# The output projection and the routing in a written order, and the first expert's weights behind the lists

## The chip, the cores and the metric

The kernel runs on one core of a Trainium2 chip. The metric is the device time of one execution in microseconds; a version is timed in several runs and their median is used. One further execution was recorded by the hardware profiler, and all rows here come from it.

## The reference

One transformer block over 1024 tokens of width 1024, in float32. The part that matters here is its end:

```python
x = x + merged @ w_out                                   # output projection
t = rms_norm(x, norm_ffn)                                # 1024 tokens
group_logits = t @ w_rg + b_rg                           # 4 groups
...                                                      # best group, softmax over its 8 experts, top 2
out = 0
for e in range(32):
    hidden = silu(t @ w_gate[e]) * (t @ w_up[e])         # width 256
    out = out + combine[:, e:e + 1] * (hidden @ w_down[e])
x = x + out
```

Each token goes to two of the 32 experts, so only these rows of `combine` are not zero.

## The kernel before

Products are made in three passes of a split float32: an operand is split into a high part (a ScalarE copy, L81) and a low part (a VectorE subtraction, L82), and `mm3` (L85 to L87) multiplies high by high, high by low and low by high.

The attention stages end with the merged branches, split, in `mT` (four pairs of buffers of the `ring`). Then the stage of this change follows, in eight token tiles `t` of 128 rows. `out_mm` projects a tile: two column halves `c`, eight steps `k` each, so 48 matmuls in all, then `x` is added (L884) and the sum `x2` stored to `out`. `w_out` comes in eight slabs `wo[k]`; the last four are loaded and split by `load_wo` shortly before. `route` squares and sums `x2` on ScalarE, takes the power -1/2 on GpSimd (L108), writes the normed rows `h2` to memory (L896, L897), transposes `x2` (L902), multiplies by the router's weights (L909), and then finds the group and the two experts in some 25 small VectorE steps and two exponentials on ScalarE. `place` counts with two small matmuls how many earlier tokens chose each expert (L959, L960) and adds the tile's entries into the slot table `psL` by two matmuls with a selection matrix `sl` (L965 to L969). After the last tile `slot_lists` makes from `psL` the lists: `ids`, the token numbers in each expert's 112 slots, and the weights `wsl`.

The experts then run one after the other. `gather` fetches an expert's rows of `h2` by an indirect DMA on GpSimd's queue into a buffer `gbuf`; four such buffers are filled with zeros first, by ScalarE (L1013). `tokens` transposes and splits the rows, `gate_up`, `hidden_t` and `down` compute, and `down` ends with an indirect DMA that adds into `out`. An expert's weights are six slabs of 512 KB, split by `weights`. They are loaded ahead: five slabs in buffers `er`, then pairs in the eight `ring` buffers as `mT` comes free after each second tile. A slab's buffer is loaded again when its low part has been made. After expert 2 a block of small VectorE steps (`ext`, `cum`, L1128 to L1141) prepares a loop over overfull experts at the end.

The order on each engine is made by the framework's scheduler from dependencies and the place in the source; engines take their queues in order, and the loads are all issued by SyncE's queue.

Of the kernel before, what the change touches and what calls it, by code (L numbers as in the profile page):

```python
# [10 lines left out]
F32 = mybir.dt.float32  # L11
# [12 lines left out]
NT = 8  # L24
# [23 lines left out]
def kernel(ctx: ExitStack, tc: tile.TileContext, a, out):  # L48
# [19 lines left out]
    def bank2():  # L68
        return psA.tile([P, 1024], F32, name="pA", tag="pA")
# [10 lines left out]
    def split(hi, lo, src, eng=None):  # L80
        nc.scalar.activation(hi, src, AF.Copy)  # L81
        (eng or nc.vector).tensor_tensor(lo, src, hi, op=ALU.subtract)  # L82
# [787 lines left out]
    X2 = {}  # L870

    def out_mm(t, k0, k1):
        if k0 == 0:
            xr = rt("xr", [P, D])
            nc.sync.dma_start(xr, a["x"][t * P:(t + 1) * P, :])
            X2[t] = (xr, bank2())
        xr, ps = X2[t]
        for c in range(2):
            o = slice(c * 512, (c + 1) * 512)
            for k in range(k0, k1):  # L880
                c_ = slice(k * P, (k + 1) * P)
                mm3(ps[:, o], mT[t // 2][0][:, t % 2, c_], mT[t // 2][1][:, t % 2, c_], wo[k][0][:, o], wo[k][1][:, o], k == 0, k == KD - 1)
            if k1 == KD:
                nc.vector.tensor_tensor(xr[:, o], ps[:, o], xr[:, o], op=ALU.add)  # L884
        if k1 == KD:
            nc.sync.dma_start(out[t * P:(t + 1) * P, :], xr)
            X2[t] = xr

    def route(t):
        x2 = X2.pop(t)  # L890
        h2 = rt("h2", [P, D])
        ss = rt("ss2", [P, 1])
        nc.scalar.activation(h2, x2, AF.Square, accum_out=ss)
        r = rt("r2", [P, 1])
        rstd(r, ss, D)
        nc.vector.scalar_tensor_tensor(h2, x2, r, gffn, op0=ALU.mult, op1=ALU.mult)  # L896
        nc.sync.dma_start(h2_d[t * P:(t + 1) * P, :], h2)  # L897
        xt = rt("xt", [P, D])
        for g in range(2):
            pt = bank()  # L900
            for k in range(4):
                nc.tensor.transpose(pt[:, k * P:(k + 1) * P], x2[:, (4 * g + k) * P:(4 * g + k + 1) * P], ident)  # L902
            if g:
                nc.vector.tensor_copy(xt[:, 512:], pt)
            else:
                nc.scalar.activation(xt[:, :512], pt, AF.Copy)
        pl = bank("g")
        for k in range(KD):
            nc.tensor.matmul(pl[:, :40], xt[:, k * P:(k + 1) * P], wrr[:, k, :], start=k == 0, stop=k == KD - 1)  # L909
# [10 lines left out]
        nc.vector.tensor_scalar(gb, gm[:, 0:1], -1.0, None, op0=ALU.mult)  # L920
        ge = rt("ge", [P, NG])
        gs = rt("gs", [P, 1])
        nc.scalar.activation(ge, lg[:, :NG], AF.Exp, bias=gb, accum_out=gs)
        sel = rt("sel", [P, NE])
        nc.vector.tensor_scalar(sel, iog, gif, NEG, op0=ALU.not_equal, op1=ALU.mult)
# [9 lines left out]
        nc.scalar.activation(ex, dl, AF.Exp)  # L935
# [5 lines left out]
        E = rt("E", [P, 2, NE])  # L941
        nc.vector.tensor_tensor(E, slots[:, None, :NE].to_broadcast([P, 2, NE]),
                                eid[:, t, :, None].to_broadcast([P, 2, NE]), op=ALU.is_equal)
# [5 lines left out]
        RT[t] = (E, L)  # L949

    RT = {}

    def place(t):

        E, L = RT.pop(t)
        M = rt("M", [P, NE], BF16)
        nc.vector.tensor_tensor(M, E[:, 0, :], E[:, 1, :], op=ALU.add)
# [3 lines left out]
        nc.vector.tensor_tensor(mcum, mcum, M, op=ALU.add)  # L961
# [10 lines left out]
    for t in range(2):  # L972
        out_mm(t, 0, 4)
    for i in range(N_RAW):
        load([er(i)])
    for t in range(2):
        out_mm(t, 4, KD)
    load_pairs(2)
    for t in range(NT):
        if 1 < t + 1 < NT:  # L980
            out_mm(t + 1, 0, KD)
            if t % 2 == 0:
                load_pairs(2)
        route(t)
        if t:
            place(t - 1)
    place(NT - 1)

    def slot_lists(ps, n, nm):


        idf = cst.tile([P, n], F32, name=f"idf{nm}")
        nc.vector.tensor_scalar(idf, ps[:, 3 * n:4 * n], ndump, dump, op0=ALU.mult, op1=ALU.add)
        ids = cst.tile([P, n], I32, name=f"ids{nm}")
        nc.vector.tensor_tensor(ids, ps[:, :n], idf, op=ALU.add)
# [5 lines left out]
    ids, wsl = slot_lists(psL, NE, "")  # L1001
    pn = bank()
# [41 lines left out]
    def tokens(e):  # L1044
# [6 lines left out]
        split(xh, xl, pt.rearrange("p (k n) -> p k n", n=P)[:, :, :BT])  # L1051
        XT[e] = (xh, xl)

# [55 lines left out]
    weights(0, 0, 6)  # L1109
    tokens(0)  # L1110
    for e in range(NE + 1):
# [7 lines left out]
        if e + 1 < NE:  # L1119
            weights(e + 1, 4, 6)  # L1120
            tokens(e + 1)
        if e:
            down(e - 1, col(ids, e - 1), col(wsl, e - 1))
        if e == 2:

            NB = 2 * S // BT + 1
            ext = pe.tile([P, NE], F32, name="ext")
            nc.vector.tensor_scalar(ext, cnt, float(BT), None, op0=ALU.is_gt)  # L1128
            for b in range(2, -(-S // BT)):
                nc.vector.scalar_tensor_tensor(ext, cnt, float(b * BT), ext, op0=ALU.is_gt, op1=ALU.add)  # L1130
            cum = [pe.tile([P, NE], F32, name=f"cum{i}") for i in range(2)]
            nc.vector.tensor_copy(cum[0], ext)
            for i, w_ in enumerate((1, 2, 4, 8, 16)):
                src, dst = cum[i % 2], cum[(i + 1) % 2]
                nc.vector.tensor_copy(dst[:, :w_], src[:, :w_])
                nc.vector.tensor_tensor(dst[:, w_:], src[:, w_:], src[:, :NE - w_], op=ALU.add)
            cm_ = cum[1]
            nbi = pe.tile([P, 1], I32, name="nbi")
            nc.vector.tensor_copy(nbi, cm_[:, NE - 1:NE])
            jc = pe.tile([P, 1], F32, name="jc")  # L1140
            nc.vector.memset(jc, 0.0)  # L1141
# [115 lines left out]
```

## Time and profile before

| | us |
|---|---|
| median of 3 runs | 1284.02 (1281.01 to 1285.81) |
| the profiled execution, its time | 1276.85 |
| its span, first to last instruction | 1275.1 |
| output projection and routing, TensorE full | 779 to 888 |
| end of the routing, lists, first gather | 888 to 911 |
| experts | 911 to 1275 |

Times in the rows are microseconds from the span's start. PE is TensorE, PEld its weight load, DVE VectorE, ACT ScalarE, POOL GpSimd, SPq SyncE's queue. A line L82 is line 82 of the kernel; helpers such as the split are used from many places, and the names of the tiles tell them apart.

### The profile page before, as it was taken

The numbers are of one execution on the slowest core, as the hardware profiler recorded it, in microseconds if no ns is written. First come the engines' busy times: TensorE is split into PE (matmuls) and PEld (weight loads), VectorE is DVE, ScalarE is ACT, GpSimd is POOL, SyncE is SP. The second block draws the span as 40 slices with busy tenths as digits, with TensorE's granted clock in tenths as the row PEclk, the third lists the DMA queues.
The fourth block names the chain that finished last, engine by engine and source line by source line (L and its number), as shares of the span: only waits on it lengthen the run. The fifth ranks groups of instructions, "written<-read, shape, count | busy, mean of one in ns | idle before, by whom it ended". The sixth has DMA issues, their size and how long they took to land.

```text
span 1275.1 us, 18222 instructions
## 1 busy us (share of the span) xinstructions
PE 1166.7 (92%) x6105; PEld 941.1 (74%) x6105; DVE 937.7 (74%) x2083; ACT 735.6 (58%) x1376; POOL 168.5 (13%) x147
## 2 busy tenths in 40 slices
PE   7789999989999999999998999999499898989994
PEld 6678888868888886777776878887377665657763
DVE  4587694368888788888764775545699788879982
ACT  6344463257667666776663443212488677668882
POOL 1000000010000001110100000000252443332112
PEclk9889999999999999999999999999599899999997
DMA  8853375383332333441215444555689999999983
GB/s 278 182 182 116 108 198 162 112 181 86 89 92 75 92 94 97 116 118 40 67 58 198 134 147 171 188 194 181 209 265 327 311 306 312 317 313 350 344 308 52
DMA packets 107615, 228.62 MB, mean 179 GB/s; under 512 B 13984, under 2 KB 47392, under 8 KB 107520
## 3 DMA queue, kind: packets, MB, share of 16 engines
q1 hardware_dynamic: 86272, 201.98, 47.7%
q0 software_dynamic: 21248, 25.46, 9.6%
q8 instruction: 49, 0.80, 0.3%
q14 instruction: 46, 0.38, 0.1%
HBM read 187.53 MB, written 52.43 MB: 188 GB/s over the span
## 4 chain that ended last, share of the span: by engine, by line
PE 49%; DMA 29%; DVE 12%; ACT 5%; issue 3%; SPq 1%; POOL 0%; POOLq 0%; ACTq 0%; DVEq 0%
DMA ring<-in_w_exp 12%; DMA er<-in_w_exp 7%; PE pG L85 6%; PE pG L86 5%; PE pG L87 5%; PE pA L85 3%; PE pB L528 3%; PE pA L86 3%; PE pA L87 3%; DMA sgl<-g_d 2%; PE pO L87 2%; PE pO L85 2%; PE pO L86 2%; DVE nbd L516 2%; PE pA L664 1%
## 5 line engine op out<-in xcount | busy, mean ns | idle before, releaser
L82 DVE TENSOR_TENSOR elo<-ring,ehi 128x1024 fp32r<-128x1024 f32 x120 | 142.4, 1220 | 16.2 <-ACT ehi L81 15.3
L81 ACT ACTIVATE ehi<-ring 128x1024 fp32r<-128x1024 f32 x120 | 124.8, 1058 | 34.7 <-DMA ring<-in_w_exp 18.3
L519 ACT ACTIVATE pd<-pA,nbd 128x512 f32<-128x512 f32 (+7 forms) x128 | 94.6, 740 | 37.8 <-DVE nbd L516 34.6
L85 PE MATMUL pG<-ring,whi 128*128 128x512 f32 x240 | 99.9, 416 | 4.5 <-ACT sg L493 4.4
L516 DVE TENSOR_REDUCE nbd<-pA 128x1 f32<-128x512 f32 (+7 forms) x128 | 95.4, 748 | 3.3 <-PE pA L567 2.6
L86 PE MATMUL pG<-ring,whi 128*128 128x512 f32 x240 | 96.3, 401 | 0.0
L87 PE MATMUL pG<-ring,wlo 128*128 128x512 f32 x240 | 95.9, 400 | 0.0
L82 DVE TENSOR_TENSOR elo<-er,ehi 128x1024 fp32r<-128x1024 f32 x72 | 85.7, 1219 | 13.5 <-ACT ehi L81 13.3
L81 ACT ACTIVATE ehi<-er 128x1024 fp32r<-128x1024 f32 x72 | 74.8, 1058 | 24.8 <-DMA er<-in_w_exp 15.0
L1092 POOL DMA_INDIRECT out<-y,ids x22 | 56.4, 2562 | 145.2 <-ACT esg L1063 30.0
L85 PE MATMUL pG<-ehi,xh 128*112 128x512 f32 x128 | 52.5, 410 | 18.6 <-ACT xh L81 18.6
L528 PE MATMUL pB<-ident,pd 128*128 128x128 f32 x432 | 66.2, 277 | 3.0 <-DVE pd L571 1.0
L528 PEld LDWEIGHTS pB<-ident,pd 128*128 128x128 f32 x432 | 48.5, 141 | 15.3 <-issue 2.7
L85 PEld LDWEIGHTS pG<-ring,whi 128*128 128x128 f32 x240 | 45.4, 189 | 17.5 <-ACT sg L493 6.7
L87 PE MATMUL pB<-ehi,ehl 128*112 128x512 f32 x128 | 53.5, 418 | 3.4 <-DVE ehl L82 3.4
L85 PE MATMUL pB<-ehi,ehh 128*112 128x512 f32 x128 | 53.6, 419 | 1.0 <-DVE y L1091 0.7
L87 PEld LDWEIGHTS pG<-ring,wlo 128*128 128x128 f32 x240 | 45.5, 190 | 10.1 <-issue 0.8
L86 PE MATMUL pO<-elo,xh 128*112 128x512 f32 x128 | 50.6, 395 | 2.5 <-DVE elo L82 2.5
L85 PE MATMUL pO<-ehi,xh 128*112 128x512 f32 x128 | 51.7, 404 | 0.7 <-ACT ehi L81 0.7
L86 PE MATMUL pB<-elo,ehh 128*112 128x512 f32 x128 | 52.1, 407 | 0.0
L87 PE MATMUL pG<-ehi,xl 128*112 128x512 f32 x128 | 51.7, 404 | 0.0
L86 PEld LDWEIGHTS pG<-ring,whi 128*128 128x128 f32 x240 | 45.6, 190 | 7.4 <-issue 1.8
(390 smaller groups left out, 3427.3 us busy)
## 6 DMA issues: line engine op xcount, KB each, us to landing
ring<-in_w_exp SPq DMA_DIRECT2D x120, 512.0 KB, 13.7
er<-in_w_exp SPq DMA_DIRECT2D x72, 512.0 KB, 13.1
er<-in_w_gate SPq DMA_DIRECT2D x16, 512.0 KB, 3.6
g_d<-sg SPq DMA_DIRECT2D x32, 256.0 KB, 2.5
sgl<-g_d SPq DMA_DIRECT2D x32, 256.0 KB, 2.8
er<-in_w_dqkv SPq DMA_DIRECT2D x8, 512.0 KB, 6.0
xT<-in_xT SPq DMA_DIRECT2D x16, 256.0 KB, 5.1
xt<-in_x SPq DMA_DIRECT2D x8, 512.0 KB, 8.3
```

Source lines behind the costliest of these rows:

```text
L81: nc.scalar.activation(hi, src, AF.Copy)
L82: (eng or nc.vector).tensor_tensor(lo, src, hi, op=ALU.subtract)
L85: nc.tensor.matmul(ps, ah, bh, start=start, stop=False)
L86: nc.tensor.matmul(ps, ah, bl, start=False, stop=False)
L87: nc.tensor.matmul(ps, al, bh, start=False, stop=stop)
L516: nc.vector.tensor_reduce(nb, ps[:, :n], axis=AX, op=ALU.max, negate=True)
L519: nc.scalar.activation(p[:, :n], ps[:, :n], AF.Exp, bias=nb, accum_out=s)
L528: nc.tensor.transpose(pt[:, (b - b0) * P:(b - b0 + 1) * P], p[:, b * P:(b + 1) * P], ident)
L664: nc.tensor.matmul(ps[f][:, k], qs[f][c], kl[c, k], start=False, stop=True)
L1092: nc.gpsimd.indirect_dma_start(out=out[:, :], out_offset=bass.IndirectOffsetOnAxis(ap=idx[:BT, :], axis=0), in_=y[:BT, :], in_offset=None, ...
```

## The change

Projection, transposes, logits, routing, counting and placing are cut into functions and written out in one order for TensorE, VectorE and ScalarE, which these three engines keep inside a `manual_schedule` block. In it, `out_mm` of tile t is interleaved with the rest of tile t-1; a tile's columns 0 to 511 are done with all k before columns 512 to 1023 begin; the square and its sum are made in two halves; the normed rows are written in two halves after the routing; `count` is split from `place`. Behind the block, the splits of expert 0's weights are issued after the last exponential (ScalarE) and after `ids` (VectorE), by `issue_after`. The zero fill of the four gather buffers moves from ScalarE to GpSimd. The block of `ext` and `cum` moves from expert 2 to expert 3 and is issued after that step's token split.

```diff
+    def out_mm(t, c, k0, k1):
...
+    def x2_half(t, c):
+        xr, ps, ss = X2[t]
+        o = slice(c * 512, (c + 1) * 512)
+        nc.vector.tensor_tensor(xr[:, o], ps[:, o], xr[:, o], op=ALU.add)
+        sq = rt("sq2", [P, 512], bufs=1)
+        nc.scalar.activation(sq, xr[:, o], AF.Square, accum_out=ss[:, c:c + 1])
+        if c == 0:
+            nc.vector.tensor_scalar(ss[:, 0:1], ss[:, 0:1], 1.0 / D, EPS, op0=ALU.mult, op1=ALU.add)
+            return
+        nc.sync.dma_start(out[t * P:(t + 1) * P, :], xr)
+        r = rt("r2", [P, 1])
+        nc.vector.scalar_tensor_tensor(ss[:, 1:2], ss[:, 1:2], 1.0 / D, ss[:, 0:1], op0=ALU.mult, op1=ALU.add)
+        nc.gpsimd.tensor_tensor(r, ss[:, 1:2], neghalf[:, :1], op=ALU.pow)
+        R2[t] = r
+    def x2_turn(t, g):
...
+        if g and t < NT - 1:
+            nc.vector.tensor_copy(xt[:, 512:], pt)
+        elif g:
+            nc.scalar.activation(xt[:, 512:768], pt[:, :256], AF.Copy)
+            nc.vector.tensor_copy(xt[:, 768:], pt[:, 256:])
+        else:
+            nc.scalar.activation(xt[:, :512], pt, AF.Copy)
+    def normed(t, o):
...
+        nc.vector.scalar_tensor_tensor(h2[:, o], x2[:, o], r, gffn[:, o], op0=ALU.mult, op1=ALU.mult)
+        if o.start:
+            nc.sync.dma_start(h2_d[t * P:(t + 1) * P, :], h2)
...
+    with tc.manual_schedule(engines={mybir.EngineType.PE, mybir.EngineType.DVE, mybir.EngineType.Activation}):
+        for t in range(NT):
+            out_mm(t, 0, 0, 3)
+            if t:
+                x2_turn(t - 1, 0)
+                x2_turn(t - 1, 1)
+            out_mm(t, 0, 3, KD)
+            if t:
+                logits(t - 1, 0, KD)
+            x2_half(t, 0)
+            out_mm(t, 1, 0, 5)
+            if t:
+                route(t - 1)
+                normed(t - 1, 0)
+                normed(t - 1, 512)
+                count(t - 1)
+            if t == NT - 1:
+                x2_turn(t, 0)
+            out_mm(t, 1, 5, KD)
+            if t:
+                place(t - 1)
+            x2_half(t, 1)
+            if t % 2:
                 load_pairs(2)
...
+        logits(t, 0, 4)
+        x2_turn(t, 1)
+        logits(t, 4, KD)
+        acted = route(t)
+        count(t)
+        normed(t, 0)
+        normed(t, 512)
+        place(t)
...
-        nc.scalar.activation(g_.rearrange("p (k n) -> p k n", n=P), slots[:, None, :].to_broadcast([P, KD, P]),
-                             AF.Copy, scale=0.0)
+        nc.gpsimd.memset(g_, 0.0)
...
-    weights(0, 0, 6)
+    with tc.issue_after(acted.ins), tc.issue_after(listed.ins):
+        weights(0, 0, 6)
...
-            tokens(e + 1)
+            turned = tokens(e + 1)
...
-        if e == 2:
+        if e == 3:
...
+            with tc.issue_after(turned.ins):
```

Inside `route`, the steps `E` and `M` now stand right behind the second exponential, and `M` no longer in `place`.

## Rows read from the trace of the kernel before

**Rows 1.** Page, DMA engines' busy tenths in 40 slices of the span

```profile
DMA  8853375383332333441215444555689999999983
```

**Rows 2.** Windows by stage: length, busy time (instructions) per engine, granted clock, DMA share

```profile
779.20:888.00 108.80, 108.79 (x559) 89.32 (x557) 53.10 (x212) 21.65 (x46) 4.32 (x10) 1.00 0.52 191
888.00:911.00 23.00, 9.39 (x54) 7.76 (x52) 20.06 (x94) 12.40 (x19) 1.90 (x3) 0.61 0.72 251
911.00:930.00 19.00, 13.67 (x61) 10.71 (x62) 9.30 (x16) 9.48 (x10) 9.64 (x9) 0.76 0.42 120
930.00:1000.00 70.00, 69.12 (x339) 51.89 (x338) 67.56 (x74) 59.13 (x74) 29.11 (x16) 1.00 0.96 320
```

**Rows 3.** Chain of waits, 755 us to the end: start, duration, what

```profile
853.03 0.87 PE pB L902 x8
...
867.28 0.87 PE pB L902 x8
...
888.11 1.72 PE pG L909 x16
...
910.78 7.14 DMA g<-h_d,ids x2
```

**Rows 4.** Timelines around w_out's last slabs: start, duration, engine, line

```profile
779.22 0.39 PE L85 MATMUL pA<-slab,ring 128*128 128x512 f32 x1
...
790.21 0.39 PE L85 MATMUL pA<-woh,ring 128*128 128x512 f32 x1
...
782.00 0.33 SPq L776 DMA_DIRECT2D er<-in_w_out  x1
...
785.84 1.06 ACT L81 ACTIVATE woh<-er 128x1024 fp32r<-128x1024 f32 x1 [3.29 <-DMA er<-in_w_out]
...
782.56 2.35 DVE L82 TENSOR_TENSOR wol<-er,woh 128x1024 fp32r<-128x1024 f32 x2
...
786.93 1.23 DVE L82 TENSOR_TENSOR wol<-er,woh 128x1024 fp32r<-128x1024 f32 x1 [1.63 <-ACT woh L81]
```

**Rows 5.** Timeline of VectorE, routing of one tile, 804 to 809 us

```profile
804.32 0.26 DVE L911 SCALAR_TENSOR_TENSOR lg<-pG,r,br 128x40 f32<-128x40 f32 x1 [1.02 <-PE pG L909]
...
808.13 0.19 DVE L957 TENSOR_TENSOR M<-E 128x32 bf16<-128x32 f32 x1
...
809.02 0.42 DVE L947 TENSOR_TENSOR L<-E,c 128x256 fp32r<-128x256 f32 x1
```

**Rows 6.** Timeline of VectorE, last tiles and lists, 891 to 909 us

```profile
891.98 0.28 DVE L968 TENSOR_SCALAR sl<-slots,pos 128x128 fp32r<-128x128 f32 x1
...
893.37 1.28 DVE L896 SCALAR_TENSOR_TENSOR h<-xr,r,gffn 128x1024 f32<-128x1024 f32 x1 [0.31 <-POOL r L108]
...
906.99 0.29 DVE L968 TENSOR_SCALAR sl<-slots,pos 128x128 fp32r<-128x128 f32 x1
...
908.20 0.19 DVE L995 TENSOR_TENSOR ids<-pO,idf 128x32 int32<-128x32 f32 x1
```

**Rows 7.** Timeline of TensorE, 892 to 897 us

```profile
892.31 0.33 PE L969 MATMUL pO<-L,sl 128*128 128x128 f32 x1 [1.46 <-DVE sl L968]
...
895.45 1.93 PE L909 MATMUL pG<-wrr,xt 128*128 128x40 f32 x8 [0.99 <-DVE xt L904]
```

**Rows 8.** Timeline of GpSimd, first gather

```profile
909.35 1.13 POOL L1040 DMA_INDIRECT ring<-h_d,ids  x1 [16.01 <-DVE ext L1130]
```

**Rows 9.** Groups of GpSimd instructions, whole span: busy us, mean ns

```profile
masks.py:197 POOL MEMSET ident<- 128x128 f32 x1 | 0.2, 205 | 0.3 <-POOLq L1247 0.3
...
L1247 POOL MEMSET const-float32-0.0<- 128x1 f32 x1 | 0.1, 99 | 0.3 <-issue 0.3
```

**Rows 10.** DMA issues, quiet 780 to 800 us, then 885 to 960 us

```profile
out<-xr SPq DMA_DIRECT2D x1, 512.0 KB, 2.6
...
h_d<-h SPq DMA_DIRECT2D x1, 512.0 KB, 4.4
```

**Rows 11.** Groups of VectorE instructions, 883.5 to 907 us: busy us, mean ns

```profile
L82 DVE TENSOR_TENSOR elo<-er,ehi 128x1024 fp32r<-128x1024 f32 x5 | 6.1, 1210 | 0.0
```

More of the change, by code (lines that the diff above doesn't have):

```diff
@@ L868, in load_pairs @@
             load([u[:, 0, :], u[:, 1, :]])
-    X2 = {}
-    def out_mm(t, k0, k1):
-        if k0 == 0:
+    X2, R2, XT2, RT = {}, {}, {}, {}
+    def out_mm(t, c, k0, k1):
+        if (c, k0) == (0, 0):
             xr = rt("xr", [P, D])
             nc.sync.dma_start(xr, a["x"][t * P:(t + 1) * P, :])
[L876 to L887, printed above, removed]
@@ L889, in route @@
-    def route(t):
[L890 to L909, printed above, removed]
+            X2[t] = (xr, bank2(), rt("ss2", [P, 2]))
@@ new lines, in x2_turn @@
+    def x2_turn(t, g):
+        x2 = X2[t][0]
+        if g == 0:
+            XT2[t] = rt("xt", [P, D])
+        xt = XT2[t]
+        pt = bank()
+        for k in range(4):
+            nc.tensor.transpose(pt[:, k * P:(k + 1) * P], x2[:, (4 * g + k) * P:(4 * g + k + 1) * P], ident)
+        if g and t < NT - 1:
[5 more added lines that the diff above has]
+            nc.scalar.activation(xt[:, :512], pt, AF.Copy)
@@ new lines, in logits @@
+    def logits(t, k0, k1):
+        if k0 == 0:
+            R2[t] = (R2[t], bank("g")) if t in R2 else (None, bank("g"))
+        xt, pl = XT2[t], R2[t][1]
+        for k in range(k0, k1):
+            nc.tensor.matmul(pl[:, :40], xt[:, k * P:(k + 1) * P], wrr[:, k, :], start=k == 0, stop=k == KD - 1)
+    def normed(t, o):
+        x2, r = X2[t][0], R2[t][0]
+        if o == 0:
+            X2[t] = (x2, rt("h2", [P, D]))
+        h2 = X2[t][1]
+        o = slice(o, o + 512)
+        nc.vector.scalar_tensor_tensor(h2[:, o], x2[:, o], r, gffn[:, o], op0=ALU.mult, op1=ALU.mult)
+        if o.start:
+            nc.sync.dma_start(h2_d[t * P:(t + 1) * P, :], h2)
@@ L934, in route @@
         ex = rt("ex", [P, 1])
-        nc.scalar.activation(ex, dl, AF.Exp)
+        last = nc.scalar.activation(ex, dl, AF.Exp)
+        E = rt("E", [P, 2, NE])
+        nc.vector.tensor_tensor(E, slots[:, None, :NE].to_broadcast([P, 2, NE]),
+                                eid[:, t, :, None].to_broadcast([P, 2, NE]), op=ALU.is_equal)
+        M = rt("M", [P, NE], BF16)
+        nc.vector.tensor_tensor(M, E[:, 0, :], E[:, 1, :], op=ALU.add)
         den = rt("den", [P, 1])
@@ L948, in route, with count @@
                                 c4[:, t, :, :, None].to_broadcast([P, 2, 4, NE]), op=ALU.mult)
[L949 to L957, printed above, removed]
+        RT[t] = (E, L, M)
+        return last
+    def count(t):
+        E, L, M = RT[t]
         pp = bank("g")
@@ L960, in place @@
         nc.tensor.matmul(pp[:, :NE], ones, mcum, start=False, stop=True)
-        nc.vector.tensor_tensor(mcum, mcum, M, op=ALU.add)
+        RT[t] = (E, L, M, pp)
+    def place(t):
+        E, L, M, pp = RT.pop(t)
         ej = rt("ej", [P, NE])
@@ L994, in slot_lists @@
         ids = cst.tile([P, n], I32, name=f"ids{nm}")
-        nc.vector.tensor_tensor(ids, ps[:, :n], idf, op=ALU.add)
+        LISTED.append(nc.vector.tensor_tensor(ids, ps[:, :n], idf, op=ALU.add))
         w = cst.tile([P, n], F32, name=f"wsl{nm}")
@@ L1001 @@
     ids, wsl = slot_lists(psL, NE, "")
+    listed = LISTED[0]
     pn = bank()
@@ L1120 @@
             weights(e + 1, 4, 6)
-            tokens(e + 1)
+            turned = tokens(e + 1)
         if e:
             down(e - 1, col(ids, e - 1), col(wsl, e - 1))
-        if e == 2:
+        if e == 3:
             NB = 2 * S // BT + 1
[L1127 to L1141, printed above, removed]
+            with tc.issue_after(turned.ins):
+                ext = pe.tile([P, NE], F32, name="ext")
+                nc.vector.tensor_scalar(ext, cnt, float(BT), None, op0=ALU.is_gt)
+                for b in range(2, -(-S // BT)):
+                    nc.vector.scalar_tensor_tensor(ext, cnt, float(b * BT), ext, op0=ALU.is_gt, op1=ALU.add)
+                cum = [pe.tile([P, NE], F32, name=f"cum{i}") for i in range(2)]
+                nc.vector.tensor_copy(cum[0], ext)
+                for i, w_ in enumerate((1, 2, 4, 8, 16)):
+                    src, dst = cum[i % 2], cum[(i + 1) % 2]
+                    nc.vector.tensor_copy(dst[:, :w_], src[:, :w_])
+                    nc.vector.tensor_tensor(dst[:, w_:], src[:, w_:], src[:, :NE - w_], op=ALU.add)
+                cm_ = cum[1]
+                nbi = pe.tile([P, 1], I32, name="nbi")
+                nc.vector.tensor_copy(nbi, cm_[:, NE - 1:NE])
+                jc = pe.tile([P, 1], F32, name="jc")
+                nc.vector.memset(jc, 0.0)
     nblocks = nc.values_load(nbi[0:1, 0:1], min_val=0, max_val=NB - 1)
```

33 lines of the change are left out of this document (13 added, 20 removed).

## Prediction

> **What bounds the kernel now.** I read the slices of the page first, then the stages around the change, then the chain of waits, then single rows. The DMA slices [rows 1] show the reader two regimes: up to about 930 us the DMA engines are half idle, and from there to 1240 us they stand at 9 nearly throughout. The stages say what is short in each [rows 2]. From 779 to 888 us, output projection and routing, TensorE is busy 108.79 of 108.80 us and DMA at 0.52: TensorE is the bound, and it has no hole to fill. From 888 to 911 us TensorE works 9.4 of 23 us and VectorE 20.1: here the routing of the last token tiles runs down on VectorE, and no expert can start. From 911 to 930 us the first rows are gathered and expert 0 begins. From 930 to 1000 us TensorE (69.1 of 70), VectorE (67.6) and DMA (0.96) are all full, and after that DMA alone carries the time.
>
> So a gain must come from the gap between the two full stretches. The time that counts is the issue of the gather of expert 0, for everything behind it is a fixed amount of work in a fixed order: 910.78 us, 22.7 us after TensorE leaves the projection at 888.11 [rows 3]. The chain of waits passes from the logits through VectorE to that gather and then 7.14 us of landing.
>
> **The change part by part.** The sum is made against the profiled execution, 1276.85 us (span 1275.1 and 1.75 around it); the median of the runs shown, 1284.02, lies 7.17 above it, and I add that at the end.
>
> *Start of the projection.* Before, tiles 0 and 1 first do their k 0 to 3 on both halves: 48 matmuls, 779.22 to 790.21, or 0.229 us each [rows 4]. That is the cover for w_out's k 4 to 7. Now tile 0 wants k 4 after 12 matmuls, at 782.0. Its parts come at fixed times, because nothing ahead of them changes: the low parts of k 5 and 6 end at 783.7 and 784.9 (two in 2.35 us from 782.56); k 7 is loaded from 782.00, split by ScalarE at 785.84 to 786.90, and its low part ends at 788.16 [rows 4]. In order, TensorE's second matmul of k 7 begins near 788.2 and the half ends 2 matmuls later, at 788.7, where 24 matmuls without a wait would end at 784.7. Cost 4.0 us. Bounds: 2.4 if VectorE took the low part of k 4 some 1.6 us sooner and so released k 7's load; 5.7 if the idle time brings the lower clock for a stretch (8 logits instructions took 1.93 us at 895.45 in the tail, where 16 took 1.72 before [rows 3, 7], and the granted clock of 888 to 911 us was 0.61 [rows 2]).
>
> *A tile's period.* The work per tile is the same: 48 matmuls, 8 transposes, 16 logits instructions, the small ones. Its period was 14.25 us (853.03 to 867.28 [rows 3]). New is where TensorE meets VectorE. Count from the end of logits(t-1). VectorE starts `lg` 0.2 later. From `lg` to `M` it took 3.81 us (804.32 to 808.13 [rows 5]); in there stand an `h` of 1.28 [rows 6] and a stray step or two, so the bare chain is 2.4. `M` is done near 2.8, and `count` reaches TensorE after 15 matmuls, at 3.5: no wait. `L` follows `M` by 0.89 [rows 5], about 1.1 (my estimate) when E and M no longer fill the gaps between dependent steps: 3.7. Then `normed`, now ahead of `place`: 0.34 for most of L, and two halves of 0.64 (half of `h`): 5.3. Then the two pairs of `ej` and `sl`, an `sl` being 0.28 [rows 6] and an `ej` less; the second `sl` starts about 0.6 on, 5.9; TensorE gets it 0.33 later (sl at 891.98, TensorE at 892.31 [rows 7]): 6.25. TensorE is there at 5.8 (24 matmuls at 0.229 and weight changes). Wait 0.45 per tile. Bounds: nothing, if VectorE's steps are together a tenth shorter; 0.9, if the first half's sum of squares, which now waits for ScalarE in front of `lg`, comes 0.4 late (add, square and read, 0.64 for each 512 columns and some 0.4 for handing over, take about 1.7 us; the logits that cover them 1.72 [rows 3]). Six such waits lie ahead of the last tile's end: 2.7 us.
>
> *The last tile.* The projection now ends with logits(6) (1.72), half the transposes of tile 7 (0.4 of the 0.87 for eight [rows 3]) and a count (0.1) already done. So TensorE leaves it at 888.1 + 4.0 + 2.7 + 2.2 = 897.0. From there, by the same 0.64: add of the last half to 0.9, square and its read to 1.8, ScalarE's quarter copy to 2.3, four logits (8 instructions, half of 1.72) to 3.3, `lg` at 3.45. Plus 3.5 to `L` (6.95), 0.34, two `normed` (8.55), `ej` and `sl` as above (second `sl` at 9.2), and 1.21 from `sl` to `ids` (906.99 to 908.20 [rows 6]): 10.4. From `ids` to the first gather's row it was 1.15 (to 909.35 [rows 8]): 11.55, so 908.6. Nothing stands between any more: before, low parts of 1.21 us (five are counted in [rows 11]; two more follow) lay between the routing's steps, the logits of tile 6 were still to do, and expert 0's gather stood behind another in GpSimd's queue [rows 3, 8]. Tail 22.7 before, 11.6 now: 11.1 gained, 8.9 of it paid ahead. Net 2.2 us.
>
> The low-clock bound for the four logits is 1.0 more. The store of h2's last rows is now late: `normed` ends at 8.65, the store lands 2.6 to 4.4 us after its issue (the quiet and the busy row of [rows 10]), 11.3 to 13.1, so it can end last by up to 1.5 us. That `ext`, which ended the first gather's wait [rows 8], is gone may give back 0.8; I take neither.
>
> *Weights behind the lists.* ScalarE's high parts start at `ex` and are done before the rows land; VectorE's six low parts take 7.3 us (at 1.21 [rows 11]) behind `ids`, hidden by the 7.14 us landing [rows 3]. Without that cover expert 0 would wait for all of it. What moves is their reload: five slabs of 512 KB, which went out while the routing still ran, now go out beside the first gathers. DMA was at 0.42 in 911 to 930 [rows 2], so they fit, but one slab (1.6 us at the 320 GB/s of a full stretch [rows 2]) is likely to share the engines with gather 0. I take 1.6; bounds 0 and 3.2, two slabs.
>
> *Zero fills on GpSimd.* The nearest row is a MEMSET of 128x128 in 205 ns against 99 for one column [rows 9]; at that slope 1024 columns cost 0.95 us, four 3.8. GpSimd is idle there (1.9 of 23 us [rows 2]), so they cost nothing if their buffers are free early in the last routing. Should the first buffer be held until the lists are made, the fills begin some 1.2 us ahead of the gather (`ids` to gather, [rows 6, 8]) and hold it for 2.6. Bounds 0 and 2.6; I take 0. The Trainium skill (SBUF — State Buffer, "Who interferes with whom") speaks against this move: VectorE's copies and tensor_scalars in a two-port mode and GpSimd share a port pair, and who comes second waits for the whole instruction. By that the sum would be 3.8 us higher, by the rows it is not; this trace has no fill of that size beside VectorE.
>
> *The block of `ext` and `cum`* (some 25 small VectorE steps, 4 to 5 us at up to 0.19 each as `M` [rows 5]) moves from VectorE's idle time to a stretch where it is 67.6 of 70 us busy [rows 2]. It can hold an expert by that; but from there DMA sets the end (0.96 [rows 2], and the nines of [rows 1]), and its queue covers a pause of 4 us as long as loads are outstanding. I take 0, bound 4.
>
> Sum: -11.1 + 8.9 + 1.6 = -0.6: 1276.25 for such an execution, 1283.4 beside the runs' median. Measurement here tells about 0.5%, 6.4 us, from no change.
>
> **Rivals.** (A) *The waits don't come*: w_out's parts are early, VectorE keeps ahead. Then 4.0 + 2.7 go, and 1 of the 1.6 for gathers: 1275.7. For it: VectorE is busy only 53 of 109 us there [rows 2], so its chains have room. Against: k 7's load cannot start before k 4 is split [rows 4]. Chance 0.25. (B) *The three fixed orders lock*: something in front of `lg` (the square's sum, a late x tile) holds VectorE, so TensorE waits at `place` in each tile. Each 1 us costs 7; from 1.0 us over my 0.45 it is slower by over 0.5%: at 1.5 us per tile 1290.8. For it: the tie of 1.7 and 1.72. Against: the same idle half of VectorE. Chance 0.17. (C) *The fills block VectorE*: if all four run beside the last tile's routing and each holds a VectorE step for its 0.95 us, the lists come 3.8 us later: 1287.2. For it nothing in these rows, against it that GpSimd has 20 idle us to put them elsewhere [rows 2]; chance 0.07. The Trainium skill's rule named above would do this. (D) *It reaches the end not at all*, because DMA's queue sets it: the idle DMA time between 888 and 945 would have to stay the same; 1284, chance 0.06. My forecast has 0.45.
>
> **How the numbers follow.** Forecast, C and D are within 0.5%: 0.58. A is faster, 0.25; B slower, 0.17. For the forecast alone 1278 to 1289 (bounds of the start -1.6 and +1.7, of the period and the store beside them). The range takes in A and most of B: 1274 to 1291.
>
> **What would show it.** Right: waits of TensorE in tile 0 on `wol` of 3 to 5 us; TensorE out of the last tile's projection 8 to 10 us later than 888; the first gather 10 to 13 us after that, near 908; DMA full from about 928. Wrong: no wait on `wol`; a period other than 14.7 us; the gather before 904 or after 912; GpSimd's fills in the chain of waits.

## The result, and the profile after

The changed kernel takes 1316.39 us (median; 1312.81 to 1322.08) against 1284.91 for the kernel before beside it: a ratio of 1.0247, 95% interval 1.0218 to 1.0276. It is slower by about 31.5 us, outside the predicted range of 1274 to 1291 and beyond the worst rival (1290.8). Its profiled execution has a span of 1316.9 us. Two kernels further below, e5 and e13, each had one execution that was far longer than all its others (1446.74 and 3949.2 us); their medians here leave that one out.

The page's slices of the changed kernel (32.9 us each), granted clock and DMA share, show the place. Slices 25 to 30, 790 to 988 us, have the clock at 7, 8, 9, 8, 6 and 8 tenths, and the nines on the DMA engines begin at 988 us, where in [rows 1] they begin at 956.

```profile
PEclk9889999989999999999999997898689989999997
DMA  7753375383333242342044433444579999999983
```

The windows by stage of the changed kernel, cut at the same events as the first two of [rows 2] (the projection, the lists); the columns are the same:

```profile
786.20:931.00 144.80, 122.47 (x584) 98.29 (x582) 64.77 (x261) 24.78 (x66) 4.31 (x10) 0.89 0.39 140
931.00:946.00 15.00, 4.07 (x28) 3.35 (x26) 11.70 (x43) 8.33 (x13) 5.98 (x6) 0.60 0.75 264
```

The first line holds the loss. The projection took 144.8 us instead of 108.8, TensorE was busy only 122.5 of them at a mean clock of 0.89, where before it had no hole at all. The tail behind it (second line) is shorter, as forecast. The chain of waits of the changed kernel names what is new:

```profile
796.12 5.83 DMA xr<-in_x
...
829.23 7.51 DMA xr<-in_x
...
863.92 8.03 DMA xr<-in_x
...
898.73 8.40 DMA xr<-in_x
...
944.22 12.67 DMA g<-h_d,ids x2
```

Four times the chain waits for an x tile (`xr`); the chain of the kernel before has no such step. SyncE's queue in the changed kernel (start, duration, line, tiles, count) says why they are late:

```profile
791.94 4.13 SPq L862 DMA_DIRECT2D er<-in_w_exp  x3
796.12 0.92 SPq L876 DMA_DIRECT2D xr<-in_x  x2
...
824.56 0.33 SPq L862 DMA_DIRECT2D ring<-in_w_exp  x1
...
825.96 0.34 SPq L893 DMA_DIRECT2D out<-xr  x1
826.35 2.79 SPq L862 DMA_DIRECT2D ring<-in_w_exp  x3
829.23 0.44 SPq L876 DMA_DIRECT2D xr<-in_x  x1
```

And the same queue in the kernel before (start, duration, line, tiles, count):

```profile
784.28 0.92 SPq L875 DMA_DIRECT2D xr<-in_x  x2
785.30 3.69 SPq L862 DMA_DIRECT2D er<-in_w_exp  x3
...
803.72 2.27 SPq L862 DMA_DIRECT2D ring<-in_w_exp  x3
806.09 0.44 SPq L875 DMA_DIRECT2D xr<-in_x  x1
...
828.05 0.33 SPq L875 DMA_DIRECT2D xr<-in_x  x1
830.87 0.33 SPq L862 DMA_DIRECT2D ring<-in_w_exp  x1
```

VectorE's first adds to the tiles loaded at 806.09 and 828.05, in the kernel before:

```profile
816.84 0.69 DVE L884 TENSOR_TENSOR xr<-pA,xr 128x512 f32<-128x512 f32 x1
...
838.82 0.69 DVE L884 TENSOR_TENSOR xr<-pA,xr 128x512 f32<-128x512 f32 x1 [0.64 <-PE pA L87]
```

Before, the first two x tiles go out ahead of the expert weights, and the later ones are asked for early: those of 806.09 and 828.05 are first added 10.8 us after their issue, although the first of them stands behind ring loads, too. After, the tiles of t = 0 and 1 stand behind three expert slabs, and those of t = 2, 4 and 6 behind the store of the tile before and four ring loads; the one at 829.23 lands 7.5 us later (the chain above), and its add waits for it. VectorE and TensorE of the changed kernel then stop in turn (each row ends with the idle time before it and its releaser):

```profile
802.05 0.69 DVE L887 TENSOR_TENSOR xr<-pA,xr 128x512 f32<-128x512 f32 x1 [5.79 <-DMA xr<-in_x]
...
836.82 0.69 DVE L887 TENSOR_TENSOR xr<-pA,xr 128x512 f32<-128x512 f32 x1 [7.47 <-DMA xr<-in_x]
```

TensorE's timeline of the same stretch, from w_out's last slabs on:

```profile
790.84 0.51 PE L86 MATMUL pA<-wol,ring 128*128 128x512 f32 x1 [0.78 <-DVE wol L82]
791.97 0.50 PE L86 MATMUL pA<-wol,ring 128*128 128x512 f32 x1 [0.17 <-DVE wol L82]
794.03 0.67 PE L85 MATMUL pA<-woh,ring 128*128 128x512 f32 x1 [1.33 <-ACT woh L81]
795.29 0.79 PE L86 MATMUL pA<-wol,ring 128*128 128x512 f32 x1 [0.59 <-DVE wol L82]
802.79 0.79 PE L85 MATMUL pA<-slab,ring 128*128 128x512 f32 x1 [6.28 <-DVE xr L887]
837.56 0.80 PE L85 MATMUL pA<-slab,ring 128*128 128x512 f32 x1 [3.80 <-DVE xr L887]
```

The first four rows are the forecast wait for w_out's last slabs, 2.9 us together: 1.5 for `wol` and, not forecast, 1.3 for `woh`. The last two are the new one: the second column half goes into the PSUM tile of the first, and starts only when VectorE has added x to the first. Over the whole stage VectorE waited for x four times, 29.3 us, and TensorE for VectorE's add four times, 18.7 us. The matmuls that follow such a pause come every 0.43 us instead of every 0.23 (granted clock 0.50 from 802.79 to 807.65), so the pause costs more than its length.

### The profile page after: what moved, and what is told of

Read it like the earlier page. It is cut to its first block, busy times and chain, and to the rows that moved or that the text cites. A ratio compares the mean times of both kernels' runs of the same rounds, so it can differ in the third digit from the quotient of the medians.

```text
span 1316.9 us, 18241 instructions
## 1 busy us (share of the span) xinstructions
PE 1177.8 (89%) x6105; PEld 946.9 (72%) x6105; DVE 946.1 (72%) x2099; ACT 733.9 (56%) x1389; POOL 179.4 (14%) x151
## 4 chain that ended last, share of the span: by engine, by line
PE 49%; DMA 28%; DVE 12%; ACT 6%; issue 3%; SPq 1%; POOL 0%; POOLq 0%; DVEq 0%; ACTq 0%
DMA ring<-in_w_exp 11%; PE pG L85 6%; PE pG L86 6%; PE pG L87 5%; DMA er<-in_w_exp 5%; PE pB L528 3%; DMA xr<-in_x 2%; PE pA L85 2%; PE pO L85 2%; PE pO L87 2%; PE pO L86 2%; PE pA L86 2%; PE pA L87 2%; DMA sgl<-g_d 2%; PE pB L87 1%
## 5 line engine op out<-in xcount | busy, mean ns | idle before, releaser
L889 ACT ACTIVATE sq<-xr 128x512 f32<-128x512 f32 x16 | 10.1, 631 | 93.2 <-DVE xr L887 93.2
L85 PEld LDWEIGHTS pG<-ring,whi 128*128 128x128 f32 x240 | 45.7, 191 | 18.7 <-ACT sg L493 7.8
```

Source lines behind the costliest of these rows:

```text
L85: nc.tensor.matmul(ps, ah, bh, start=start, stop=False)
L889: nc.scalar.activation(sq, xr[:, o], AF.Square, accum_out=ss[:, c:c + 1])
```

## The experiments

In the expectations, the third, fourth and ninth kernels are e3, e4 and e9 below. Since stages ahead of the change moved the projection's start between 779 and 788 us from one profiled execution to the next, positions are counted from there: S is the start of the first `pA<-slab` matmul, and the table gives, from rows of each trace, the issue of expert 0's gather, the first transposes of gathered rows, the transposes of expert 0's hidden values (`ehd`), and the end of the span. A position comes from one execution; e14, which is as fast as before, ends at 497.6 against 495.9, so 1 to 2 us between two traces mean little.

| kernel | median us | ratio to before, 95% interval | gather | rows | ehd | end |
|---|---|---|---|---|---|---|
| before (beside the others 1280.7 to 1285.9) | 1284.9 | | 131.6 | 136.9 | 148.8 | 495.9 |
| after | 1316.4 | 1.0247 [1.0218, 1.0276] | 158.0 | 167.1 | 181.8 | 530.7 |
| e1_x_first | 1294.7 | 1.0066 [1.0044, 1.0088] | 136.5 | 145.8 | 160.3 | 508.3 |
| e2_halves | 1313.3 | 1.0194 [1.0161, 1.0228] | 149.7 | 158.4 | 173.3 | 524.1 |
| e3_x_first_cover | 1292.2 | 1.0047 [1.0030, 1.0064] | 132.2 | 141.3 | 156.6 | 504.8 |
| e4_lists_only | 1286.4 | 0.9993 [0.9964, 1.0022] | 124.1 | 132.9 | 150.6 | 497.8 |
| e5_free_splits | 1291.8 | 1.0057 [1.0036, 1.0078] | 137.7 | 142.2 | 155.3 | 504.6 |
| e7_fill_scalar | 1291.6 | 1.0054 [1.0031, 1.0077] | 134.0 | 142.7 | 158.0 | 504.5 |
| e8_gather_alone | 1290.7 | 1.0047 [1.0027, 1.0066] | 132.2 | 137.2 | 150.5 | 504.8 |
| e9_normed_behind_place | 1290.8 | 1.0039 [1.0020, 1.0057] | 131.2 | 139.8 | 154.2 | 500.9 |
| e12_pipeline_probe0 | 1291.0 | 1.0047 [1.0025, 1.0068] | 132.2 | 136.8 | 149.9 | 503.5 |
| e14_before_x_late | 1284.5 | 0.9996 [0.9974, 1.0018] | 131.8 | 136.7 | 150.6 | 497.6 |
| e11_lists_probe0 | 1282.7 | 0.9981 [0.9962, 1.0000] | 124.1 | 129.3 | 145.7 | 495.8 |
| e13_lists_probe1 | 1283.4 | 0.9988 [0.9964, 1.0012] | 124.0 | 129.4 | 146.0 | 496.6 |
| e15_before_fewer | 1264.0 | 0.9865 [0.9845, 0.9886] | 131.6 | 136.9 | 149.1 | 479.3 |
| e16_lists_fewer | 1263.8 | 0.9878 [0.9844, 0.9912] | 124.1 | 129.1 | 146.2 | 477.0 |
| e17_pipeline_fewer | 1273.5 | 0.9943 [0.9921, 0.9965] | 132.7 | 138.4 | 154.7 | 492.0 |

**Is it the late x tiles?** e1 loads the x tiles ahead of the expert weights.

```diff
+    load_x(0)
+    load_x(1)
     for i in range(N_RAW):
         load([er(i)])
...
                 normed(t - 1, 512)
+                if t < NT - 1:
+                    load_x(t + 1)
                 count(t - 1)
```

> The changed kernel, but the x tiles are loaded ahead of the expert weights in SyncE's queue: tiles 0 and 1 before the five slabs, tile t+1 right behind the normed rows of tile t-1, so ahead of the four ring loads. Theory 1 (the queue: x of tiles 0, 2, 4, 6 lands late, and TensorE waits for the add): TensorE's four waits on the add (18.7 us idle, more with the lower clock) go, the stage from the first projection matmul to the last falls from 144.6 us to 116 to 121, the time to 1289 to 1294. Rival 2 (the written order itself locks the three engines in every tile): nothing or up to 5 us better, 1311 to 1316. Rival 3 (weights behind the lists and their reload beside the gathers carry the loss): at most 5 us better as well.

1294.66 us: 21.7 of the 31.5 us come back by moving eight DMA issues. VectorE's wait for x fell from 29.3 us to 0.7. The time lies just above the expected range, and the projection (123.2 us from the first to the last matmul's start) lies above its 116 to 121, so other losses remain behind the late x tiles.

**Or the PSUM tile that the halves share?** e2 leaves x late and gives each half its own tile.

```diff
-            X2[t] = (xr, bank2(), rt("ss2", [P, 2]))
+            X2[t] = (xr, [bank2(), bank2()], rt("ss2", [P, 2]))
...
-            mm3(ps[:, o], mT[t // 2][0][:, t % 2, c_],
+            mm3(ps[c][:, :512], mT[t // 2][0][:, t % 2, c_],
```

> The changed kernel, but each column half of the projection has a PSUM tile of its own, so that the second half's matmuls need not wait for the add that reads the first half; x stays late. If TensorE's waits come only through the shared PSUM tile: all of second halves runs on, until count needs the routing's M; each late tile gives back up to 3.4 us (15 matmuls), tile 0 up to 5.5, in all 8 to 15 us: 1301 to 1308. If the late x itself holds VectorE's order (theory 1), the small matmuls wait instead: 3 to 8 us better. Rival 2: no change, 1316.

1313.28: 3.1 us by the medians, with intervals that overlap, where 8 to 15 were expected if the shared tile were the cause. VectorE still waits 29.1 us for x. TensorE no longer waits for the add, but a step later. The waits of TensorE in e2 (waited for, us in total, times, longest):

```profile
PE pG L986 <- DVE M L968: 12.9, 3, 4.7
```

That is `count`, which needs a routing step that is queued on VectorE behind the add. With three written orders, removing one meeting place moves the wait to the next; of these two changes only that of the late transfer was worth making.

**The start.** e3 is e1 with k 0 to 3 of tiles 0 and 1 done first, on both halves, as before.

```diff
+        for t in range(2):
+            for c in range(2):
+                out_mm(t, c, 0, 4)
         for t in range(NT):
-            out_mm(t, 0, 0, 3)
+            if t > 1:
+                out_mm(t, 0, 0, 3)
```

> As the one with the x tiles first, and tiles 0 and 1 do k 0 to 3 of both halves first, as before the change, to cover w_out's last slabs. Theory 1 with my start term: the 4 to 5 us of waits on the low parts of w_out go, 1285 to 1290, and the stage takes 112 to 116 us. If the start were covered otherwise: as the x-first kernel.

1292.19, above the expected 1285 to 1290, and 2.5 us less than e1 by medians whose intervals overlap; the trace tells more. The last projection matmul comes 4.4 us earlier from S (118.8 against 123.2), but the cover brings waits of its own in tiles 0 and 1, 3.1 us together. The two longest in TensorE's timeline of e3:

```profile
800.94 0.50 PE L85 MATMUL pA<-woh,ring 128*128 128x512 f32 x1 [0.78 <-DVE xr L891]
...
812.68 0.18 PE L990 MATMUL pG<-M,tri 128*128 128x32 bf16 x1 [2.02 <-DVE M L972]
```

**The other half of the change alone.** e4 is the kernel before with expert 0's splits behind the lists, and nothing else.

```diff
-    weights(0, 0, 6)
+    with tc.issue_after(acted.ins), tc.issue_after(LISTED[0].ins):
+        weights(0, 0, 6)
```

> The kernel before, with one part of the change alone: the splits of expert 0's weights are issued behind the last exponential and behind ids. If these splits had only been in the way: the lists come 7 to 8 us earlier, the gather lands 3 to 5 us slower beside the reloads, 1280 to 1283 against 1285. If the weights behind the lists cost (rival 3): the first expert starts later, 1288 to 1295.

No difference in time, between the two expected ranges. The gather starts 7.5 us earlier, its rows come 4.0 earlier, and at expert 0's `ehd` the kernel is already 1.8 us late. So an earlier gather need not be an earlier first expert, which asks where the gain goes.

**What keeps the repaired pipeline above before?** Four variations of e3, with the following edits: e5 takes the two `issue_after` off expert 0's splits; e7 puts the zero fills back on ScalarE; e8 holds the five reloads that these splits free until the first later ring load has been issued; e9 moves `normed` of tiles 0 to 6 behind `place`.

```diff
# e5
-    with tc.issue_after(acted.ins), tc.issue_after(listed.ins):
-        weights(0, 0, 6)
+    weights(0, 0, 6)
# e7
-        nc.gpsimd.memset(g_, 0.0)
+        nc.scalar.activation(g_.rearrange("p (k n) -> p k n", n=P), slots[:, None, :].to_broadcast([P, KD, P]),
+                             AF.Copy, scale=0.0)
# e8
-                load(unit)
+                load(unit, e == 0)
...
+                last = load_pairs(1)
+                if LATE:
+                    with tc.issue_after(last.ins):
+                        while LATE:
+                            nc.sync.dma_start(*LATE.pop(0))
# e9
-                normed(t - 1, 0)
-                normed(t - 1, 512)
...
                 place(t - 1)
+                normed(t - 1, 0)
+                normed(t - 1, 512)
```

> The third kernel (x tiles early, cover for w_out's last slabs; 1292.2 us) with expert 0's splits left free to mix into the routing, so that the buffers they empty are loaded again some 7 us earlier, ahead of the last normed tile's store in SyncE's queue. Theory 4 (the stretch from the first expert to the end, 363.6 us there against 359.0 before, is set by when the reloads start): 1286 to 1289 us. Theory 5 (what is left is the first gather's landing, 9.1 us after its issue against 5.4 before, and the wait at place): the reloads only move ahead of the store that the gather needs, 1291 to 1294 us.

> The third kernel with the zero fills of the gather buffers back on ScalarE (Copy with scale 0) instead of GpSimd. If GpSimd's fill stretches VectorE's one-hot of the last tile (0.94 us beside it against 0.29 without) and holds the gather's start, the gather comes 0.7 to 1.5 us earlier: 1290.5 to 1291.5 us. If the first gather waits for nothing of that: 1292 us. On ScalarE the fills may stand before the split's rounding: up to 1 us the other way.

> The third kernel with the five reloads that expert 0's splits free issued only behind the first ring load that follows them, so that the first gathers have the DMA engines with fewer weight loads beside them. If the loads beside it make the first gather slow (9.1 us from issue to the first transpose against 5.4 before): it lands in 5.5 to 7 us, 1288 to 1290 us. If the gather is slow because GpSimd writes its descriptors slowly beside VectorE's splits: still 9 us, 1292 us, or up to 1297 us where the reloads, some 10 us later, set the end (theory 4).

> The third kernel with the normed rows of tiles 0 to 6 (two 0.6 us instructions of VectorE) behind the tile's placing instead of ahead of it, so that TensorE no longer waits 0.54 us for the one-hot rows in each tile: 1288.5 to 1289.5 us if that wait is what makes a tile 14.8 us instead of 14.25 (6 x 0.54 = 3.2 us). If VectorE's work only moves ahead of the next tile's add and TensorE waits there: 1292 us and a period of 14.8 us as before.

None differs from e3 by more than the timing can tell (1290.7 to 1291.8 against 1292.2), so no time here decides between its two expectations, yet the traces do differ. In e5 the five reloads begin earlier (four at S+123, ahead of the last `h_d` store, instead of S+132), but the gather starts 5.5 us later; the time lies in theory 5's range. In e7 the selection matrix `sl` takes 0.28 us again, but the fills now follow the splits on ScalarE and hold the gather, which starts 1.8 us later. In e9 the place wait goes, but the x tiles, asked for behind `normed`, are now asked for behind `place`, too, and VectorE's add waits for x in four tiles, 16.4 us in all; TensorE feels little of that (it waits 2.5 us for the add, 0.8 in e3). e8 tells most. First transposes of gathered rows in e3:

```profile
927.52 1.73 PE L1112 MATMUL pA<-ident,g 112*128 112x112 f32 x8 [11.21 <-DMA g<-h_d,ids]
931.35 1.35 PE L1112 MATMUL pA<-ident,g 112*128 112x112 f32 x6 [2.11 <-DMA g<-h_d,ids]
```

And in e8:

```profile
919.15 1.73 PE L1124 MATMUL pA<-ident,g 112*128 112x112 f32 x8 [7.12 <-DMA g<-h_d,ids]
921.52 1.35 PE L1124 MATMUL pA<-ident,g 112*128 112x112 f32 x6 [0.65 <-DMA g<-h_d,ids]
```

Counted from the gathers at 918.47 and 914.18, the rows are there after 9.0 us in e3 and after 5.0 in e8, and the second pair of transposes waits 0.65 instead of 2.11. The reloads beside the gather are what makes it slow (the runs with held reloads further below agree). At `ehd` e8 is 6.1 us ahead of e3 (150.5 against 156.6) and still ends at the same 504.8: with the reloads some 20 us later (from 934.54, S+153), the rest took 6 us longer.

**Does a queue order alone cost 22 us?** e14 is the kernel before with the x tiles behind the expert loads, as in the changed kernel.

```diff
-    for t in range(2):
-        out_mm(t, 0, 4)
     for i in range(N_RAW):
         load([er(i)])
+    for t in range(2):
+        out_mm(t, 0, 4)
...
-            out_mm(t + 1, 0, KD)
-            if t % 2 == 0:
+            if t % 2:
                 load_pairs(2)
+            out_mm(t + 1, 0, KD)
```

> The kernel before, with only the order of SyncE's queue changed to that of the kernel after: the x tiles of tiles 0 and 1 behind the three expert-weight loads of the start, and the ring loads of a pair of tiles ahead of the next tile's x load instead of behind it. Theory 1 (the queue's order costs by itself): TensorE or VectorE waits for late x tiles here too; the planner may move other work into the gaps, so 5 to 22 us more than before, 1291 to 1308 us. The rival (the late x tile costs only where three engines run in a fixed order): 1284 to 1289 us.

1284.51, no cost, in the rival's range. SyncE's queue of e14 (start, duration, line, tiles, count), and VectorE's first add to the tile loaded at 831.81:

```profile
787.85 4.04 SPq L862 DMA_DIRECT2D er<-in_w_exp  x3
791.94 0.92 SPq L875 DMA_DIRECT2D xr<-in_x  x2
...
831.81 0.33 SPq L875 DMA_DIRECT2D xr<-in_x  x1
833.97 1.76 SPq L862 DMA_DIRECT2D ring<-in_w_exp  x4
...
841.91 0.69 DVE L884 TENSOR_TENSOR xr<-pA,xr 128x512 f32<-128x512 f32 x1 [0.65 <-PE pA L87]
```

The two x tiles of the start stand behind the expert slabs here, too. VectorE waits 6.3 us for them, and TensorE never waits for the adds. But all later x tiles still go out 10 us or more ahead of their first add, as they do before. So two late x tiles at the start cost nothing where the scheduler makes the order; x tiles that are late in the middle of the stage were not tried in that order. Whether the queue's order alone makes the 22 us, or the asking for x in the tile that uses it, stays open: e1 changed both.

**Can the earlier gather be made to count?** e11 is e4 with the reloads held until the first gathered tile has landed, by a 32-byte copy of it in SyncE's queue; e13 takes the copy from the second tile; e12 does as e11 with e9.

```diff
+    seen = pe.tile([1, 8], F32, name="seen")
+    landed = nc.sync.dma_start(seen, gused[0][:1, :8])
+    with tc.issue_after(landed.ins):
+        while LATE:
+            nc.sync.dma_start(*LATE.pop(0))
     tokens(0)
```

> The kernel before with expert 0's splits behind the lists (as in the fourth kernel, whose gather started 7.5 us earlier and then took 8.9 us instead of 6.8), and the five reloads that these splits free held in SyncE's queue behind a copy of 32 bytes of the first gathered tile, so that they start when it has landed. If the reloads beside it make the gather slow and the end follows the first transposes: gather lands 5 to 6 us after its issue, first transposes some 130 us after the projection's start (136.9 before), 1277 to 1281 us. If the end follows the reloads: 1285 to 1290 us.

> As the kernel before it in this list, with the copy taken from the second expert's gathered tile, so that the reloads also wait for the second gather, whose transposes came 2 us late beside reloads: if the second gather matters too, 1 to 2 us less than with the first, 1276 to 1280 us; if the reloads' time sets the end, 1 to 2 us more.

> The ninth kernel (pipeline, x tiles early, cover at the start, normed rows behind place; 1290.8 us) with the reloads of expert 0's buffers held behind the first gather's landing. First transposes 5 us after the gather's issue instead of 8.6, reloads 5 us later: 1286 to 1288 us if the end follows the first transposes, 1290 to 1294 us if it follows the reloads.

In e11 the rows are there at 129.3, 7.6 us ahead of before, as expected; the time is 1282.66, between the two expected ranges, at most 0.4% better and perhaps nothing (the interval reaches 1.0000). At `ehd` 3.1 of the 7.6 us are left, for reasons seen in TensorE's timeline of e11:

```profile
915.06 0.77 PE L85 MATMUL pO<-ehi,xh 128*112 128x512 f32 x1 [1.07 <-ACT xh L81]
...
919.89 0.63 PE L87 MATMUL pG<-ehi,xl 128*112 128x512 f32 x1
920.32 0.48 PE L85 MATMUL pG<-ehi,xh 128*112 128x512 f32 x1
920.64 0.39 PE L86 MATMUL pG<-elo,xh 128*112 128x512 f32 x1
```

Until 920.32 matmuls follow each other at 0.43 us, then at 0.23: the lower clock lasted 11 us from the first transposes here, 4 us before. At the ninth expert 1.8 of the 3.1 us are left (`ehd` at 224.1 against 225.9), at the end 0.1. e13 does no better than e11. e12 lies in the range expected if the end follows the reloads: it is 4.3 us ahead of e9 at `ehd` but ends 2.6 later, with its reloads held 7 us longer.

**Are the loads the bound of the experts' stage?** The last three leave some of the loads into the `er` buffers out (their experts then compute with older contents of the buffer), in the kernel before, in e11 and in e9. The expectations count 25; by the traces it is 24, 48 issues instead of 72.

```diff
             RAW[ej] = (slab_, unit, left)
+            if len(unit) == 1 and ej[0] >= 3 and ej[0] % 3 == 0:
+                continue
```

> The kernel before with 25 of the expert-weight loads into the single buffers (those of every third expert from the third on) left out; the splits and matmuls stay and read what the buffer held, so the outputs of those experts are wrong. 25 x 0.52 MB at some 0.32 MB per us are 41 us of transfers. If the loads set the end of the routed stage: faster by 15 to 30 us (TensorE's own idle time there, some 25 us, is the limit), 1255 to 1270 us. If TensorE sets it: 1282 to 1286 us.

> The kernel before with expert 0's splits behind the lists and the reloads held behind the first gather (whose first transposes came 7.6 us earlier, with a time 0.2% below before), and the same 25 loads left out. If the loads swallowed the earlier gather: 4 to 8 us faster than the kernel before with fewer loads. If the later stretch would have lost it anyway: the same as that one within 2 us.

> The ninth kernel (repaired pipeline, 1290.8 us; first transposes 2.9 us later than before, counted from the projection's start) with the same 25 loads left out. If the later loads are the reason for its 5.6 us: the gap to the kernel before with fewer loads shrinks to the first transposes' 2 to 4 us. If the pipeline loses time elsewhere: the gap stays at 5 to 6 us.

e15: 1263.95 us, 17 us (1.35%) less with every matmul in place, as the loads' theory expected. From S+200 to S+450 TensorE is idle 8.4 us where it was idle 25.0 before. So the loads set the pace there, for these 17 us at least.

e16 did not give the 4 to 8 us expected if the loads swallowed the earlier gather: it stands within 2 us of e15, the range expected if the later stretch loses the lead anyway. In its trace it keeps the lead that e11 lost (2.9 us at `ehd`, 2.9 at the ninth expert, 2.3 at the end), but the intervals of about 0.3% are wider than such a lead. So that the loads swallowed the earlier gather is not shown.

e17 missed both ranges: it stayed 9.5 us above e15, more than e9 above before; 5.6 of that are there at `ehd`, the rest arises later and stays open. Three of the five reloads beside its first gather are among those left out, and its rows come 5.7 us after the issue where those of e9 take 8.6.

## Why the prediction was wrong

*The failed step* is the costing of a tile's period: "New is where TensorE meets VectorE." It followed each compute step of the written order and took the add of x as ready when its matmuls are. `out_mm` also issues the load of its x tile, and the source now has that call behind the three `er` loads and behind `load_pairs`, and in the tile that uses x instead of one ahead. Nothing in the sum prices that; the late x tile appears only as an example in rival B, priced as 1.5 us in each tile where it was up to 8.2 us of VectorE's time in every second one. e1 shows it: 21.7 us.

*The start* was right in size: 4.0 forecast, and the first half of tile 0 ends 4.4 us later than 24 matmuls without a wait (the last of them starts at 795.88 instead of 791.5). Of these 2.9 are waits; the rest goes with slower matmuls there (0.50 to 0.79 us instead of 0.39), which stood among the bounds as the lower clock. What came behind was not forecast: tile 0's second half waits for the add of its first (2.3 us in e1), and nothing of a tile before it covers that.

*The place wait* was right: 0.45 forecast; without late x a tile of e3 takes 14.79 us (from 819.11 to 833.90, the transposes of two tiles) against 14.25 before, so 0.54. Taking it away (e9) returned 1.4 us by the medians, which the timing cannot tell from nothing.

*The tail* was right in kind and short in size: from the end of the projection to the gather 13.2 us (931.0 to 944.22) where 11.55 was forecast and 22.7 was there before (888.11 to 910.78 [rows 3]). VectorE's timeline of the changed kernel's last tile answers to [rows 5, 6]:

```profile
934.67 0.26 DVE L939 SCALAR_TENSOR_TENSOR lg<-pG,r,br 128x40 f32<-128x40 f32 x1 [0.94 <-PE pG L921]
...
938.22 0.42 DVE L977 TENSOR_TENSOR L<-E,c 128x256 fp32r<-128x256 f32 x1
938.56 1.41 DVE L930 SCALAR_TENSOR_TENSOR h<-xr,r,gffn 128x512 f32<-128x512 f32 x2
...
940.11 0.94 DVE L999 TENSOR_SCALAR sl<-slots,pos 128x128 fp32r<-128x128 f32 x1
...
941.12 0.29 DVE L999 TENSOR_SCALAR sl<-slots,pos 128x128 fp32r<-128x128 f32 x1
...
942.32 0.19 DVE L1047 TENSOR_TENSOR ids<-pO,idf 128x32 int32<-128x32 f32 x1
...
942.53 1.22 DVE L82 TENSOR_TENSOR elo<-er,ehi 128x1024 fp32r<-128x1024 f32 x1
943.66 0.18 DVE L1050 TENSOR_TENSOR wsl<-pO,wsl 128x32 f32<-128x32 f32 x1
```

`lg`, `L` and the two `h` come within 0.4 us of the forecast. The first `sl` takes 0.94 instead of 0.28 (below). Another 0.75 us are a low part that slips in between `ids` and the last step of `wsl`, behind which the profile puts the gather: an order that holds a split behind `ids` alone leaves the rest of the lists behind the split.

*The gather beside the reloads* was undersized: 1.6 us forecast with a bound of 3.2; the rows came 9.1 us after the issue (944.22 to 953.28) where before they took 5.4 (910.78 [rows 3] to the first transposes at S+136.9, 916.1), and 5.0 where e8 held the reloads back. The 7.14 us that the sum took for the landing is a row of two gathers (x2); the first rows were there earlier.

*The fills* were given nothing with a bound of 2.6: they cost 0.66 us, one `sl` beside one fill. So rival C named the way, at a sixth of its price. The fill's price, 0.95 us by the slope of two small ones, was right (0.95). *`ext` and `cum`* were given nothing: from the fourth to the sixth expert's `ehd` e9 takes 24.8 us where before takes 23.3, so 1.5 us; TensorE waits there 0.31 us for `xh` and 1.05 for `ehl`, while these steps stand in VectorE's queue. At the end of e9 that is gone again.

*That a gain of the gather reaches the end* was the assumption under the whole sum, "everything behind it is a fixed amount of work in a fixed order". The reloads are part of that work, and they moved: those of expert 0's buffers went from S+116 to S+132 in e3, where x is early. e4, e11 and e13, with gathers 7.5 us earlier and little or no time to show for it, fit rival D, which had 0.06, but do not show it: most of their lead is gone at expert 0's `ehd`, and e11's interval holds both no gain and the 3.1 us that were left. The best sign for it is e8, 6.1 us ahead of e3 at `ehd` with its reloads some 20 us later, and not ahead at the end. In the kernel before the DMA engines run at 0.92 to 0.99 from S+150 to S+450.

*What is left with the x tiles early*: in e1, counted from S, the projection ends 5.8 us after its forecast place (123.6 against 117.8), the tail is 1.3 us longer than forecast, the rows take 2.3 us more than forecast to land, and from the rows to the end it takes 3.5 us more than before. With the start covered and the place wait gone (e9) 5.0 us by the medians remain; in its trace 5.4 are there at expert 0's `ehd`: 2.9 when the first rows come, the rest from the second gather's late rows and a longer stretch at the lower clock. How much of this each costs at the end stays open.

## What to carry to other kernels

A step that is moved in the source takes its DMA issues along: list, for each queue, what it now stands behind and when that can leave, before costing a single matmul. Where engines keep a written order, ask for every load well ahead of its use (here 10.8 us ahead went unnoticed, and a load that was asked for at its use cost up to 8.2 us), because no engine can fill the gap with other work. And before a gap ahead of a saturated stage is closed, read what saturates that stage: if it is loads, as e15 shows here in part, an earlier start of compute may be worth no more than the loads it brings forward (e8 points that way; the times do not prove it).

## What the runs showed of the hardware

A gather of 112 rows was ready for TensorE 4.5 to 5.3 us after its issue when no weight load was issued beside it (e8, e11, e12, e13, e16), 5.7 us with two loads of 512 KB beside it (e17), and 8.6 to 9.3 us with five (e1, e2, e3, e4, e7, e9, after). GpSimd's instruction took 1.84 us in e8 and e11 as well, against 1.00 before, so its own length is not the cause.

VectorE's 128x128 `sl` took 0.94 us instead of 0.28 while a fill ran on GpSimd. GpSimd's timeline of the changed kernel:

```profile
940.03 0.95 POOL L1066 MEMSET g<- 128x1024 f32 x1 [4.72 <-DVE h L930]
942.10 0.95 POOL L1066 MEMSET g<- 128x1024 f32 x1 [1.13 <-PE pB L1056]
944.22 1.74 POOL L1092 DMA_INDIRECT g<-h_d,ids  x1 [1.17 <-DVE wsl L1050]
```

`sl` began at 940.11 and ended with the fill; with the fills on ScalarE (e7) it took 0.28. This agrees with the Trainium skill (SBUF — State Buffer, "Who interferes with whom"), which has VectorE's two-port modes and GpSimd wait for each other for a whole instruction. `ids`, which ran beside the second fill, kept its 0.19 us.

After the pause before the experts, matmuls ran at 0.43 us each for 4 us in the kernel before and for 11 us in e11, where the rows came earlier but with more pauses between them (granted clock 0.50 in these 11 us, 0.99 in the 10 us behind): the earlier start was partly paid back in the lower of the two levels, 1.2 against 2.4 GHz.
